# Merge gates of two token blocks computed as ten steps of seven block products between the mLSTM and the merge

## The chip, the cores and the metric

One core of a Trainium2 chip runs the whole kernel. The metric is the time of one execution in microseconds (us); lower is better. A core has five engines: TensorE (PE, matrix products into PSUM), VectorE (DVE), ScalarE (ACT), GpSimd (POOL) and SyncE (SP), which here issues every DMA of the kernel from one queue, in program order.

## The reference, cut to what matters

One layer over 2048 tokens of width 1024. Three mixers (a bidirectional mLSTM, a 2-D neighbourhood attention, a cross-attention into 256 memory tokens) work on one normalised input `h`; sigmoid gates computed from the same `h` merge them; an MLP follows.

```
h = rmsnorm(x, g_mix)
z = h @ w_in                                   # w_in: 1024 x 5648
qk_m, v_m, o_m, i_pre, f_pre, qkv_na, q_mem, gate_pre = split(z)
h_m, h_na, h_mem = mlstm(...), neighbourhood_attention(...), memory_cross_attention(...)
gates = sigmoid(gate_pre).reshape(bsz, s, 3, 1024)   # gate_pre: 3072 of the 5648 columns
y = (gates[:, :, 0] * (h_m @ w_proj_mlstm) + gates[:, :, 1] * (h_na @ w_proj_na)
     + gates[:, :, 2] * (h_mem @ w_proj_mem))
x = x + y @ w_out
return x + square(relu(rmsnorm(x, g_ffn) @ w_up)) @ w_down
```

## The kernel before, in words

Everything is float32. A product is made of three matmuls (`mm3`, L235 to L237): each operand is split into a rounded high part and a low remainder, and high x high, high x low and low x high are added in PSUM. The splits of the weights are an ACT copy and a DVE subtraction (L179/L180 in `fetch`, L205/L206 in `fetch_sums`). Raw weights arrive in tiles `wr`, their split parts are `ws`.

The tokens are four blocks of 512 (b = 0 to 3). `hT` holds one block's normalised input, transposed and split. The PE's order is the program's order; DVE, ACT, POOL and SP are ordered by a scheduler when the program is built, and each then runs in that order. A "tick" is a call between two groups of six matmuls; at each tick, generators ("streams") put in a piece of side work.

Stage one (`phase_1`, `block_a` once for each block) makes the projections of `h`, and its side streams do the attention (`na_stream`) and the memory branch. One attention head of a tile of 128 queries is a score matmul (L1086), a DVE operation that adds the bias and takes the maximum (L1089), an ACT exponential (L1091), a DVE reciprocal and scaling (L1093, L1094), transposes on PE (L1105) and their copy (L1110 on DVE or L1108 on ACT); there are 128 of these. `NA_RATE` says at how many of four ticks a head is put in: one in blocks 0 to 2, two in block 3. The attention's keys, queries, values and biases are loaded from DRAM as `nak`, `naq`, `nav`, `nab`.

A gate unit j (of 24) is 128 columns of the gate weights against one block: 24 matmuls of 128x512, a tanh on ACT (L608) and a store to `s_g`. Blocks 2 and 3 make all their 48 units in stage one (`GATES_1`); blocks 1 and 0 make theirs in stage two, as the filling between the pieces of the mLSTM (`phase_2`, `ml_stream`); what is left of them when the mLSTM is done follows at once (`late_gates`). `sums_down` prepares combinations of the down weights (16 calls, in stage one; loads `xt`, four DVE subtractions L588, stores `s_t`).

Stage three (`phase_3`): for two pairs of blocks, (3, 2) and (1, 0), the merge, the output projection, and the MLP in products of a 2x2 block scheme with seven products instead of eight (`mlp_up`, `mlp_down`). `load_mix` loads a block's three branch outputs (8 DMAs of 512 KB). `X` and `B` hold the operands of the seven products.

The mLSTM runs over 32 chunks (16 in each direction), one in a slot of four ticks, after a start of `START_2` = 20 ticks in which the gates' log-sigmoids (`ml_logsig`) and the first rows of running sums and maxima (`ml_rows`: loads `r_f` and `r_i`, scans L757 and L763, subtractions L766 and L767, PE transposes L784) are made. The seven products of one step stand in `mlp_up` like this (eight would be 96 matmuls, seven are 84):

```
product(c11, "a11", "b11", True)
product(p6, "s2", "t2", True)
product(c12, "s1", "t1", True)
product(c21, "s3", "t3", True)
product(c12, "s4", "b22", False)
product(c11, "a12", "b21", False)
product(c21, "a22", "t4", False)
```

Of the kernel before, what the change touches and what calls it, by code (L numbers as in the profile page):

```python
# [24 lines left out]
TB = 512  # L25
LOW, LATER, LATER_A, SOON = 100, 60, 60, 40
START_2, ROWS_2 = 20, 8
ALONE = 6
CUT = 384
# [3 lines left out]
PREP_V = 2  # L33
MEM_T, MEM_R = 6, 3
NA_LATER, NA_VALUES = 5, 3
# [11 lines left out]
GATES_1, GATES_2 = [2, 3], [1, 0]  # L47
SPILL = [0, 1]
NA_RATE = {0: 1, 1: 1, 2: 1, 3: 2}
# [34 lines left out]
class Body:  # L84
    def __init__(self, tc, a):
# [4 lines left out]
        self.na_ready, self.na_end, self.na_rate, self.tk = [], False, 1, 0  # L90
# [53 lines left out]
    def plan(self):  # L144

        u = unit_index()
        self.down = u["down"]
        out = list(u["w_mem_kv"])
        for b in range(NB):
            for n in ("naqk", "qk", "navm", "v"):  # L150
                out += u[n]
            if b in GATES_1:
                out += u["gate"]
            out += u["o"]
        out += u["gate"] + u["gate"][:ALONE]
        up = [(u["up"][j][0], u["up"][j + 1][0], "sums") for j in range(0, FF // 128, 2)]
        return out + (u["proj"] + u["w_out"] + up) * (NB // 2)

# [132 lines left out]
    def scratch(self):  # L291
# [19 lines left out]
            hT={b: d(f"s_hT{b}", [128, 2, 8, TB]) for b in SPILL},  # L311
            x2=[d(f"s_x2{b}", [TB, D]) for b in range(NB)],
# [62 lines left out]
    def phase_1(self):  # L375
# [7 lines left out]
        self.streams = [self.unit_stream(self.qkq, [(1, 3)]), self.unit_stream(self.memq, [(0,), (2,)]), self.na_stream()]  # L383
# [24 lines left out]
    def prep_x(self, gsrc=None, xt=None):  # L408

        if self.xorder:  # L410
# [81 lines left out]
    def block_a(self, b):  # L492
# [20 lines left out]
        for c in range(4):  # L513
            self.conv(b, c, self.ch_group(self.take(1)[0], hT))
        w = self.take(4)
        zif = self.t("zif", [128, 4, 16], 1)
        for t in range(4):
# [4 lines left out]
            for half in range(2):  # L522
                for r in range(2):
                    p0 = r * 64 + half * 24
                    self.store(self.scr["vna"][half, 8 * b + 2 * t + r], s[p0:p0 + 40])
            p = self.tok_group(hT, w, t, slice(256, 528), 4)
# [4 lines left out]
        for g in {0: [0], 1: [1, 2], 2: [3, 4], 3: [5, 6, 7]}[b]:  # L531
            self.na_ready.append(g)
        self.jobs += [None, None, lambda: self.if_rows(b, zif)]
        w, sums = self.take(4), None
        for t in range(4):
            if t == PREP_V and b + 1 < NB and b not in GATES_1:
# [5 lines left out]
            if b == NB - 1 and t % 2 == 0:  # L542
                sums = sums or self.sums_down(15)
                sums = next(sums, None) and sums
        if b in GATES_1:
            sums, qs = None, list(range(7)) if b + 1 < NB else list(range(7, 15))
            for j in range(24):
                if j == 22 and b + 1 < NB:
                    self.prep_x()
                self.gate(b, j)  # L550
                if j < 21 or b + 1 == NB:
                    if j % 3 != 2:
                        sums = sums or self.sums_down(qs.pop(0))
                        sums = next(sums, None) and sums
        gml = self.gbc[:, b % 2 * TB:(b % 2 + 1) * TB]
        nc.sync.dma_start(gml, a["g_mlstm"])
        w = self.take(4)
        for t in range(4):
# [9 lines left out]
            if b == NB - 1:  # L568
                ts = slice(t * 128, (t + 1) * 128)
                src = self.scr["hT"][GATES_2[0]]  # L570
                if t < 3:
                    nc.sync.dma_start(hT[:, :, :, ts].bitcast(F32), src[:, :, :, ts])
                else:
                    for k in range(0, 8, 2):
                        for l in range(2):
                            nc.sync.dma_start(hT[:, l, k:k + 2, ts].bitcast(F32), src[:, l, k:k + 2, ts])

    def sums_down(self, q):
# [3 lines left out]
        r = [self.x_tile(self.a["w_units"][self.down[half * FF // 256 + q][0]]) for half in range(2)]  # L582
# [1040 lines left out]
```

## Time and profile before

| | |
|---|---|
| time, median of 3 runs | 2893.73 us (2888.53 to 2898.1) |
| profiled execution: time, span | 2894.83 us, 2893.1 us |
| PE busy, weight loads busy | 2861.0 us, 2364.8 us |
| DVE, ACT, POOL busy | 2004.3, 1187.3, 216.4 us |
| DMA | 632.79 MB, mean 219 GB/s |
| stage one, first block of gates in stage two, stage three | from 0, from 938, from 1302 us |

Busy time of PE counts a matmul from its start to a modelled end, and matmuls overlap, so 99% busy does not say that there is nothing to save. What a matmul costs is read from the distance of starts: the profile's rows with `x1` give the start in the first column and the duration in the second.

### The profile page before, as it was taken

How to read it: one execution, taken by the hardware profiler on the slowest of the kernel's cores; microseconds unless marked ns; L12 is line 12 of the kernel's file. 1: busy time of each engine (PE TensorE's matmuls, PEld its weight loads, DVE VectorE, ACT ScalarE, POOL GpSimd, SP SyncE). 2: the span in 40 equal slices, each digit the busy share in tenths (PEclk: the TensorE clock that was granted, in tenths of full speed). 3: DMA queues.
4: the chain of work that ended last, by engine and by line, in shares of the span. 5: the costliest groups of instructions: out<-in, count | busy, mean ns of one | idle time of the engine just before them, and what ended most of it. 6: DMA issues, size and time to landing. Idle time of an engine off the chain costs nothing.

```text
span 2893.1 us, 41875 instructions
## 1 busy us (share of the span) xinstructions
PE 2861.0 (99%) x15052; PEld 2364.8 (82%) x15052; DVE 2004.3 (69%) x3438; ACT 1187.3 (41%) x2256; POOL 216.4 (7%) x382
## 2 busy tenths in 40 slices
PE   8999999999999999999999999999999999999999
PEld 6878788878877888888888888888888888888887
DVE  6676765567765555647598888666785988885666
ACT  7465654344543443532243334443322433344331
POOL 4121310011000122310000000000000000000000
PEclk9999999999999999999999999999999999999999
DMA  8786778877899888978344446656863444476654
GB/s 281 227 270 203 226 231 259 259 222 231 270 306 299 269 258 283 308 261 272 117 137 158 160 146 238 224 189 228 301 205 113 144 148 160 151 249 202 196 188 160
DMA packets 345153, 632.79 MB, mean 219 GB/s; under 512 B 29456, under 2 KB 151248, under 8 KB 344944
## 3 DMA queue, kind: packets, MB, share of 16 engines
q1 hardware_dynamic: 344944, 630.10, 67.5%
q8 instruction: 119, 1.95, 0.3%
q14 instruction: 90, 0.74, 0.1%
HBM read 453.37 MB, written 176.62 MB: 218 GB/s over the span
## 4 chain that ended last, share of the span: by engine, by line
PE 89%; DVE 3%; issue 3%; DMA 3%; ACT 1%; POOL 0%; SPq 0%; DVEq 0%; POOLq 0%; ACTq 0%
PE mm L235 27%; PE mm L237 27%; PE mm L236 27%; PE tr L1105 1%; PE pn L882 1%; PE mx L1086 1%; PE mx L1119 1%; PE pn L885 1%; PE mx L891 1%; DVE ws L180 1%; DMA nav<-s_vna 1%; PE mx L1258 1%; PE tr L1248 1%; DMA xt<-in_xT_dram 0%; DMA wr<-in_w_units_dram 0%
## 5 line engine op out<-in xcount | busy, mean ns | idle before, releaser
L235 PE MATMUL mm<-X,ws 128*128 128x512 f32 x896 | 349.0, 389 | 0.0
L237 PE MATMUL mm<-X,ws 128*128 128x512 f32 x896 | 348.6, 389 | 0.0
L236 PE MATMUL mm<-X,ws 128*128 128x512 f32 x896 | 348.6, 389 | 0.0
L180 DVE TENSOR_TENSOR ws<-wr,ws 128x1024 fp32r<-128x1024 f32 (+1 forms) x194 | 240.0, 1244 | 127.4 <-ACT ws L179 126.2
L235 PE MATMUL mm<-hT,ws 128*128 128x512 f32 (+1 forms) x712 | 283.0, 397 | 0.7 <-ACT ev L565 0.7
L237 PE MATMUL mm<-hT,ws 128*128 128x512 f32 (+1 forms) x712 | 277.0, 389 | 0.0
L236 PE MATMUL mm<-hT,ws 128*128 128x512 f32 (+1 forms) x712 | 276.7, 389 | 0.0
L235 PE MATMUL mm<-ws,hT 128*128 128x512 f32 (+2 forms) x704 | 258.3, 367 | 3.5 <-ACT zif L529 2.7
L237 PE MATMUL mm<-ws,hT 128*128 128x512 f32 (+2 forms) x704 | 249.6, 355 | 2.2 <-DVE hT L438 2.2
L179 ACT ACTIVATE ws<-wr 128x1024 fp32r<-128x1024 f32 (+1 forms) x194 | 204.1, 1058 | 111.1 <-PE mm L237 76.0
L236 PE MATMUL mm<-ws,hT 128*128 128x512 f32 (+2 forms) x704 | 248.7, 353 | 0.0
L237 PE MATMUL mm<-X 128*128 128x512 f32 x616 | 239.7, 389 | 0.2 <-DVE X L1509 0.2
L236 PE MATMUL mm<-X 128*128 128x512 f32 x616 | 239.6, 389 | 0.0
L235 PE MATMUL mm<-X 128*128 128x512 f32 x616 | 239.6, 389 | 0.0
L205 ACT ACTIVATE ws<-wr 128x512 fp32r<-128x512 f32 x224 | 135.0, 628 | 220.1 <-PE mm L237 139.5
L1508 ACT ACTIVATE X<-X 128x1024 fp32r<-128x1024 f32 x109 | 115.6, 1062 | 202.6 <-DMA X<-s_a 67.2
L237 PEld LDWEIGHTS mm<-X,ws 128*128 128x128 f32 x896 | 168.2, 188 | 35.0
L235 PEld LDWEIGHTS mm<-X,ws 128*128 128x128 f32 x896 | 168.2, 188 | 34.9
L236 PEld LDWEIGHTS mm<-X,ws 128*128 128x128 f32 x896 | 168.2, 188 | 34.8
L1509 DVE TENSOR_TENSOR X<-X 128x1024 fp32r<-128x1024 f32 x109 | 132.6, 1223 | 79.0 <-ACT X L1508 78.5
L1535 DVE TENSOR_TENSOR acc<-acc,mm 128x512 f32<-128x512 f32 x192 | 126.5, 683 | 64.8 <-PE mm L237 64.8
L235 PEld LDWEIGHTS mm<-hT,ws 128*128 128x128 f32 x712 | 134.0, 188 | 28.9 <-issue 4.3
(286 smaller groups left out, 5985.6 us busy)
## 6 DMA issues: line engine op xcount, KB each, us to landing
wr<-in_w_units_dram SPq DMA_DIRECT2D x290, 512.0 KB
s_s<-u SPq DMA_DIRECT2D x32, 1024.0 KB
s_g<-ev SPq DMA_DIRECT2D x96, 256.0 KB
ev<-s_g SPq DMA_DIRECT2D x96, 256.0 KB
s_a<-u SPq DMA_DIRECT2D x96, 256.0 KB
X<-s_s SPq DMA_DIRECT2D x45, 512.0 KB
nab<-in_rpb_dram SPq DMA_DIRECT2D x96, 220.0 KB
xt<-in_w_units_dram SPq DMA_DIRECT2D x32, 512.0 KB
```

The source lines that it names most:

```text
L179: nc.scalar.activation(w[:, 0], raw, AF.Copy)
L180: nc.vector.tensor_tensor(w[:, 1], raw, w[:, 0].bitcast(F32), ALU.subtract)
L205: nc.scalar.activation(hi, src, AF.Copy)
L235: mm(out, lhs[0], rhs[0], start=first, stop=False)
L236: mm(out, lhs[0], rhs[1], start=False, stop=False)
L237: mm(out, lhs[1], rhs[0], start=False, stop=last)
L882: mm(pn[h % 2][:, h // 2], pt[:, h], v1[:, h], start=h < 2, stop=first)
L885: mm(pn[h % 2][:, h // 2], qw[hp, h // 2], C[hp, h // 2], start=False, stop=True)
L891: nc.tensor.matmul(pu[hp, h // 2], kw[:, h], v1[:, h], start=True, stop=True)
L1508: nc.scalar.activation(hi, src, AF.Copy)
L1509: nc.vector.tensor_tensor(lo, src, hi.bitcast(F32), ALU.subtract)
L1535: nc.vector.tensor_tensor(c, c, p, ALU.add)
```

## The change

The gate units are placed anew: block 0 keeps its place in stage two, block 3 is made at the end of stage one and in stage two, and most of blocks 1 and 2 is made late, as a pair:

- Stage one makes 4 units (`EARLY`) of blocks 1 and 2 and, at its end, 8 units (`FIRST_3`) of block 3: 16 units instead of 48. Stage two makes 16 units of block 3 and 24 of block 0: 40 instead of 48.
- The other 20 units of blocks 2 and 1 are made after the mLSTM and before the merge, in `pair_gates`: ten steps, each two units against two blocks in seven products of 12 matmuls. Its weights are prepared by `fetch_sums`, as in `mlp_up`; its right-hand operands are made from the normalised input of blocks 1 and 2, which stage one now stores (`s_raw`, 8 DMAs of 512 KB) and which is loaded again in stage two (`load_raw`, 4 DMAs of 1 MB) and combined and split (`gate_operands`: 22 DVE and 14 ACT operations of 128x1024).
- Block 1's spilled `hT` (4 MB out, 4 MB in) is gone; block 0's stays.
- The attention is put in at two of four ticks in blocks 1 to 3, and at three of four in block 3 after its value projection; the order of the projections changes (`navm` ahead of `qk`).
- Of the 16 `sums_down`, 11 stay in stage one (six of them in block 3), five move into `pair_gates`.
- The mLSTM's slots have three ticks, except slots 20 to 31; it starts after 11 ticks, since `ml_logsig` moves to the end of stage one.
- `load_mix` for the first pair moves from the start of stage three into the last steps of `pair_gates`.

In all there are 24 x 40 + 24 x 16 + 10 x 84 = 2184 gate matmuls instead of 2304.

The diff, cut to its core:

```diff
-START_2, ROWS_2 = 20, 8
-ALONE = 6
-CUT = 384
+START_2, ROWS_2 = 11, 0
+FIRST_3, EARLY, ALONE = 8, 4, 4
-NA_LATER, NA_VALUES = 5, 3
+NA_LATER, NA_VALUES, NA_HOLD = {1: 5, 2: 5, 3: 4}, {1: 3, 2: 3, 3: 2}, 3
-GATES_1, GATES_2 = [2, 3], [1, 0]
-SPILL = [0, 1]
-NA_RATE = {0: 1, 1: 1, 2: 1, 3: 2}
+GATES_2, GATES_3 = [3, 0], [2, 1]
+SPILL = [0]
+NA_AT = {1: (3,), 2: (1, 3), 3: (1, 2, 3)}
+NA_RATE = {0: 1, 1: 2, 2: 2, 3: 2}
+SUMS_1 = {0: 1, 1: 2, 2: 2, 3: 6}
...
     def block_a(self, b):
...
+        if b == NB - 1:
+            self.na_rate = 3
...
+        if b == NB - 1:
+            for j in range(FIRST_3):
+                if j == 2:
+                    self.ml_logsig()
+                self.gate(b, j)
+                sum_step()
...
     def late_gates(self, more):
...
+            if i == 1 and new and self.raw is None:
+                self.load_raw()
...
     def ml_stream(self):
...
+            ticks = 3 if slot < 20 or slot >= 32 else 4
...
     def phase_3(self):
...
-        for j in range(2):
-            self.load_mix(order[j], mix[j])
         nc.sync.dma_start(self.gbc, a["g_ffn"])
+        self.jobs += self.gate_operands()
         self.late_gates(lambda: True)
+        while self.jobs:
+            self.tick()
...
+        first[0] = self.pair_gates(order[0], order[1], first[1])
...
+    def load_raw(self):
+        raw = self.p_h.tile([128, 2, 8, TB], F32, name="raw", tag="hT", bufs=1)
+        for h in range(2):
+            for j, b in enumerate(GATES_3):
+                x = raw[:, j, 4 * h:4 * h + 4]
+                self.raw[f"b{h + 1}{2 - j}"] = x
+                self.nc.sync.dma_start(x, self.scr["raw"][b][:, 4 * h:4 * h + 4])
...
+    def gate_operands(self, late=False):
...
+        split("b11", b11)
+        split("b22", b22)
+        op(b12, b22, b12, ALU.subtract)
+        op(b11, b12, b11, ALU.add)
+        split("t2", b11)
+        split("t3", b12)
+        op(b22, b22, b11, ALU.subtract)
+        split("t1", b22)
...
+    def pair_gates(self, b0, b1, mix1):
...
+        for n, j in enumerate(pairs):
+            w, = self.take(1)
+            c11, p6, c12, c21 = (self.ps("mm") for _ in range(4))
+            u2, u3, p5, o11 = (self.ev() for _ in range(4))
+            product(w, c11, "a11", "b11", True)
+            nc.scalar.activation(u2, c11, AF.Copy)
+            if n == len(pairs) - 1:
+                self.load_mix(b1, mix1, (1,))
+            product(w, p6, "s2", "t2", True)
+            add(u2, u2, p6)
+            product(w, c12, "s1", "t1", True)
+            nc.scalar.activation(p5, c12, AF.Copy)
+            if n == len(pairs) - 1:
+                self.load_mix(b1, mix1, (0,))
+            product(w, c21, "s3", "t3", True)
+            add(u3, u2, c21)
+            add(p5, u3, p5)
+            out(p5, c2, j + 1)
+            if sums:
+                next(sums.pop(0), None)
+            product(w, c12, "s4", "b22", False)
...
```

Three places in the built order. The first is SP's queue at the border of stages one and two. Before, the rows' loads `r_f` stand behind the store of the log-sigmoids `s_lf` and three loads of block 0's operand `hB`:

```order
786 L623 DMA hB<-s_hT_156 128x2x512 [waits DMAHW3_49]
787 L623 DMA hB<-s_hT_156 128x2x512 [waits DMAHW4_49]
788 L105 DMA s_lf<-ev_10795 128x128 [waits DMAHW5_49,DVE_49]
789 L105 DMA s_g_93<-ev_10861 128x512 [waits DMAHW6_49,Activation_49]
790 L175 DMA wr_10899<-in_w_units_dram 128x1024 [waits DMAHW7_49]
791 L623 DMA hB<-s_hT_156 128x2x512 [waits DMAHW0_49]
792 L753 DMA r_f<-s_lf 4x512 [waits DMAHW5_49,DMAHW1_49,Pool_49]
```

After, in the same queue:

```order
690 L107 DMA s_t_200<-xt_9503 128x2x512 [waits DMAHW2_49,DMAHW1_49,DVE_49]
691 L107 DMA s_t_200<-xt_9505 128x2x512 [waits DMAHW3_49]
692 L107 DMA s_g_95<-ev_9658 128x512 [waits Activation_49]
693 L181 DMA wr_9728<-in_w_units_dram 128x1024 [waits DMAHW4_49,DVE_49]
694 L181 DMA wr_9771<-in_w_units_dram 128x1024 [waits DMAHW6_49,DMAHW5_49,DVE_49]
695 L774 DMA r_f<-s_lf 4x512 [waits DMAHW3_49,DMAHW7_49,PE_49,Pool_49]
```

The rows' loads now stand right behind the last stores of stage one: a down-weight combination (`s_t`) and the last gate of stage one (`s_g`).

The second is DVE in block 3, where the attention is densest. `nsb` is a head's scores, `npt` its transposed weights, `ws` a weight split, `nho` an output. Before:

```order
1159 L1093 RECIPROCAL sm_9974<-sm_9972 128x1
1160 L1094 TENSOR_SCALAR nsb_9969<-nsb_9969,sm_9974 128x320
1161 L180 TENSOR_TENSOR ws_9912<-wr_9911,ws_9912 128x8x128
1162 L1126 TENSOR_TENSOR nho_9347<-mx_10005,nho_9347 128x4x32
1163 L1110 COPY npt_10032<-tr_10028 120x384
1164 L1089 ISA nsb_10036,sm_10037<-mx_10034,nab_0_1_0_9906 128x320
```

After:

```order
1041 L1122 RECIPROCAL sm_8499<-sm_8497 128x1
1042 L1118 ISA nsb_8518,sm_8519<-mx_8516,nab_0_1_2_8348 128x440
1043 L1118 ISA sm_8519 128x1
1044 L1123 TENSOR_SCALAR nsb_8494<-nsb_8494,sm_8499 128x440
1045 L606 TENSOR_TENSOR xt_8249<-xt_8249,xt_8251 128x512
1046 L1122 RECIPROCAL sm_8523<-sm_8521 128x1
1047 L1118 ISA nsb_8544,sm_8545<-mx_8542,nab_0_1_3_8397 128x440
```

Two heads are now open at a time on DVE, and a subtraction of the down weights (`xt`), which needs a load, stands between them.

The third is DVE late in the mLSTM, where `pt` and `kw` are a chunk's score weights, `og` and `h` the chunk three slots older, `C` the state. Before:

```order
1641 L863 TENSOR_TENSOR kw_2566_13919<-sk_2518_13711,de_2551_13851 128x256 [waits DMAHW0_49,Pool_49]
1642 L866 TENSOR_TENSOR pt_2556_13886<-sk_2518_13711,de_2551_13851 128x512
1643 L926 TENSOR_TENSOR h_2536_13793<-og_13805,rs_13802 128x512 [waits Pool_49]
1644 L924 TENSOR_TENSOR og_13913<-og_13913,h_2561_13901 128x512 [waits DMAHW2_49,DVE_49]
1645 L180 TENSOR_TENSOR ws_13830<-wr_13829,ws_13830 128x8x128 [waits DMAHW3_49,Activation_49]
```

After:

```order
1610 L884 TENSOR_TENSOR kw_2491_12773<-sk_2442_12555,de_2476_12705 128x256 [waits Pool_49]
1611 L887 TENSOR_TENSOR pt_2481_12740<-sk_2442_12555,de_2476_12705 128x512
1612 L1371 TENSOR_TENSOR raw<-raw 128x1024 [waits DMAHW5_49,DMAHW3_49]
1613 L1371 TENSOR_TENSOR raw<-raw 128x1024
1614 L945 TENSOR_TENSOR og_12659<-og_12659,h_2461_12647 128x512 [waits DMAHW7_49]
```

The first operation on the reloaded input (`raw`) stands among the chunk's own operations, and waits for its loads, four of 1 MB each, which stand in a row in SP's queue.

More of the change, by code (lines that the diff above doesn't have):

```diff
@@ L89, in __init__ @@
         self.streams, self.qkq, self.memq, self.aux_end = [], [], [], False
-        self.na_ready, self.na_end, self.na_rate, self.tk = [], False, 1, 0
+        self.na_wait, self.done, self.na_end, self.na_rate, self.tk = list(range(8)), set(), False, 1, 0
+        self.down_q = list(range(16))
         self.na_v, self.na_vfree = [], 2
@@ L311, in scratch @@
             hT={b: d(f"s_hT{b}", [128, 2, 8, TB]) for b in SPILL},
+            raw={b: d(f"s_raw{b}", [128, 8, TB]) for b in GATES_3},
             x2=[d(f"s_x2{b}", [TB, D]) for b in range(NB)],
@@ L541, in block_a @@
             self.store(self.scr["v"][b][t * 128:(t + 1) * 128], s)
[L542 to L548, printed above, removed]
+            if b == NB - 1:
+                sum_step()
+        if b in GATES_3:
+            for j in range(EARLY):
+                if j == EARLY - 2:
                     self.prep_x()
                 self.gate(b, j)
[L551 to L555, printed above, removed]
+                if j < 2:
+                    sum_step()
         nc.sync.dma_start(gml, a["g_mlstm"])
@@ L660, in ml_stream @@
             live[d] = [None if c is None else self.ml_chunk(d, c)] + live[d][:3]
-            for tick in range(4):
-                for age in when[tick]:
+            for tick in range(ticks):
+                for age in when[3 if tick == ticks - 1 else tick]:
                     if age < len(live[d]) and live[d][age]:
                         next(live[d][age], None)
-                if tick < 3:
+                if tick < ticks - 1:
                     next(rows, None)
@@ L1292, in phase_3 @@
                 self.hT = self.p_h.tile([128, 2, 8, TB], F32R, name="yT", tag="hT", bufs=1)
-            yT = [[self.hT[:, l] for l in range(2)], [planes("b21"), planes("t4")]]
+                yT0 = [self.hT[:, l] for l in range(2)]
+            else:
+                yT0 = [planes("t3"), planes("b22")]
+            yT = [yT0, [planes("b21"), planes("t4")]]
             self.ahead = 4
-            self.merge(pair, mix, yT)
+            self.merge(pair, mix if i else first, yT)
             self.out_proj(pair, yT)
```

196 lines of the change are left out of this document (137 added, 59 removed).

## The prediction

> **What bounds the kernel now.** I read the page's busy table first, then the stretches of the stages, then what PE waited for, then the starts of matmuls.
>
> ```profile
> span 2893.1 us, 41875 instructions
> PE 2861.0 (99%) x15052; PEld 2364.8 (82%) x15052; DVE 2004.3 (69%) x3438; ACT 1187.3 (41%) x2256; POOL 216.4 (7%) x382
> ```
>
> A matmul's busy time is modelled and overlaps its neighbours', so 99% says only that PE hardly ever stands still. How little it waits is in the view of waits, for PE alone (total us, times, longest):
>
> ```profile
> PE mx L235 <- ACT ws L179: 7.4, 1, 7.4
> PE mx L1086 <- ACT me L1236: 3.6, 2, 1.8
> PE mx L1086 <- DMA nak<-s_ks: 3.4, 2, 2.2
> PE mm L235 <- ACT zif L529: 2.7, 3, 1.3
> ```
>
> The largest is the start of the program, and all that follow are a few microseconds. The price of a matmul comes from stretches (us, busy us and count of PE, PEld, DVE, ACT, POOL; clock; DMA share; GB/s): stage one, stage two, stage three, then a piece of the MLP with nothing but products, and the busiest 100 us of block 3.
>
> ```profile
> 0.00:937.00 937.00, 914.01 (x5801) 756.47 (x5802) 619.16 (x1370) 484.64 (x1014) 139.63 (x251) 1.00 0.81 252
> 937.00:1302.00 365.00, 363.58 (x2215) 299.31 (x2214) 201.76 (x429) 152.30 (x479) 76.78 (x131) 1.00 0.86 276
> 1302.00:2893.00 1591.00, 1583.37 (x7040) 1309.05 (x7038) 1183.40 (x1640) 550.35 (x765) 0.00 (x0) 1.00 0.56 186
> 1500.00:1800.00 300.00, 300.00 (x1325) 248.43 (x1324) 250.06 (x377) 101.47 (x159) 0.00 (x0) 1.00 0.50 170
> 800.00:900.00 100.00, 96.41 (x634) 78.30 (x635) 65.58 (x159) 46.61 (x99) 3.80 (x27) 1.00 0.98 304
> ```
>
> Products alone: 300 us hold 1325 matmuls that touch the stretch, each 0.39 us long, so the starts are (300 + 0.4) / 1325 = 0.2267 us apart, not 0.389. DVE is 250 of 300 us busy there (83%) with PE never waiting. The granted clock is 1.00 throughout. So PE binds in every stage, and whatever takes matmuls away without a new wait shortens the span at 0.2267 us each.
>
> **The change part by part. Products.** Gate matmuls fall from 2304 to 2184: 120 x 0.2267 = **-27.2 us**. It depends little on where they stand. In stage one a gate with one head in it runs between these two rows (start, duration):
>
> ```profile
> 555.29 0.40 PE L235 MATMUL mm<-hT,ws 128*128 128x512 f32 x1
> 560.80 0.60 PE L1105 MATMUL tr<-ident,nsb 128*120 128x128 f32 x4
> ```
>
> 24 matmuls in 5.51 us, 0.2296 each. Moving 960 of them (40 units) out of stages one and two at 0.2296 and putting 840 back at 0.2267 gives 220.4 - 190.4 = -30.0. The 0.07 us more per gate comes with the head, and the heads stay, so I take -27.2 and keep -30.0 as the far end. The 24 matmuls in two pieces (`CUT`) become whole ones; that is counted. The moved stores, weights and tanhs are as many as before or fewer, except 20 more loads for ten sets of sums against 34 fewer single units; ACT at 41% hides its part.
>
> **Denser attention in block 3.** Stage one loses 32 gates, the cover under which heads run. Per head:
>
> ```profile
> L1091 ACT ACTIVATE nsb<-nsb,sm 128x440 f32<-128x440 f32 (+1 forms) x128 | 81.6, 638 | 94.6 <-DVE sm L1089 92.2 <-DVE halo L684 0.9
> L1089 DVE CUSTOM_DVE_ANT_0 nsb<-mx,nab 128x440 f32<-128x440 f32 (+1 forms) x128 | 73.9, 578 | 58.5 <-PE mx L1086 43.3 <-POOL nsb L1097 8.5 <-DMA nab<-in_rpb_dram 4.3
> L1094 DVE TENSOR_SCALAR nsb<-nsb,sm 128x440 f32<-128x440 f32 (+1 forms) x128 | 55.2, 432 | 3.1
> L1110 DVE COPY npt<-tr 120x512 f32<-120x512 f32 (+1 forms) x64 | 41.7, 652 | 33.0 <-PE tr L1105 32.9
> L1093 DVE RECIPROCAL sm<-sm 128x1 f32<-128x1 f32 x128 | 20.4, 159 | 40.2 <-ACT nsb L1091 39.9
> ```
>
> DVE has 0.578 + 0.432 + 0.159 + 0.652 / 2 = 1.50 us per head. Three heads in four ticks are 24 x 0.2267 = 5.4 us of products and about 2.7 us of the heads' own PE work (0.65 each between the two gates above, from 6.16 us per gate and head, and the values), 8.1 us: one head per 2.7 us, DVE 55% busy with heads. For now, the same stretch 800 to 900 has this many of L1094 (us, DVE busy, count):
>
> ```profile
> 800.00:900.00 100.00, 10.76 (x26) 1.00 0.98 304
> ```
>
> 26 heads, one per 3.85 us, take 39 of DVE's 65.6 us, all else 27. Block 3 lasts from about 600 to 912 us; without 16 of its 24 gates (87 us) and with some heads already done in blocks 1 and 2, I estimate 205 us, so all else would weigh 1.5 times as much, 40%, less 8 weight splits and 3 of 9 sums (8 x 1.24 + 12 x 0.69 = 18 us, 9%): 31%. Together 86%, a little over the 83% under which PE has been seen not to wait. The loads grow as well:
>
> ```profile
> nab<-in_rpb_dram SPq DMA_DIRECT2D x96, 220.0 KB
> nak<-s_ks SPq DMA_DIRECT2D x36, 352.0 KB
> naq<-s_qs SPq DMA_DIRECT2D x48, 128.0 KB
> nav<-s_vna SPq DMA_DIRECT2D x24, 180.0 KB
> ```
>
> A head needs 220 KB of bias, an eighth of 3 x (352 + 128) and a quarter of 180: 445 KB, 0.456 MB: 169 GB/s at 2.7 us against 118 GB/s at 3.85. With the rest as now, 304 GB/s (share 0.98) become some 355. The 48 dense heads last 130 us; 45 GB/s too many are 5.9 MB, 19 us at 304 GB/s. From below it is nothing, as weights are fetched five units ahead and can wait. Between 0 and +19 I take **+5**, nearer the 3.4 us that `nak` costs at 0.98 now.
>
> [...]
>
> **The border of stages one and two.** The rows now start at once instead of 13 us later. Before (start, duration; SP, DVE, PE, POOL):
>
> ```profile
> 951.25 0.35 SPq L753 DMA_DIRECT2D r_f<-s_lf  x1
> 962.15 0.68 DVE L766 TENSOR_TENSOR r_i<-r_i,r_b 36x512 f32<-36x512 f32 x1
> 965.75 0.22 PE L784 MATMUL mx<-ident,r_m 4*128 4x4 f32 x1
> 938.27 0.44 PE L235 MATMUL mm<-hT,ws 128*128 128x384 f32 x1 [0.69 <-ACT ev L565]
> 941.81 0.52 POOL L712 MEMSET r_i<- 36x512 f32 x1 [39.90 <-DMA hT<-s_hT]
> ```
>
> From the issue of `r_f` to the end of L766 it is 11.6 us, then PE may transpose. PE comes to these transposes 11 ticks into the stage, 66 x 0.2267 = 15.0 us. The row tiles are cleared by POOL only when stage one's buffers are free, 3.5 us into the stage before (941.81 - 938.27, waiting for a DMA), and five clearings of 0.5 us follow; `r_f` could be issued about 5 us in and PE served at 16.6: +1.6 us. With the last `s_t` store a few us late it is +6.6; if nothing is late, 0. I take **+3**. PE's own queue stands behind that wait, so the gates wait as well, and `hB`, which now has 8 ticks less to land, profits from it.
>
> **The reloaded input.** DVE's first operation on `raw` stands between two chunks' work and needs 3 of 4 MB that are issued about two slots ahead, when DMA is as full as it gets. 4.2 MB at 304 to 330 GB/s are 13 us, two slots are 13 to 16. Loads of the next chunks queue behind it. Nothing to +6, since a chunk's own loads have a slot of slack; I take **+2**.
>
> **Operands for the first step.** 16 ticks of one DVE operation each, and a first set of sums:
>
> ```profile
> L1509 DVE TENSOR_TENSOR X<-X 128x1024 fp32r<-128x1024 f32 x109 | 132.6, 1223 | 79.0 <-ACT X L1508 78.5
> L206 DVE TENSOR_TENSOR ws<-wr,ws 128x512 fp32r<-128x512 f32 x224 | 151.1, 687 | 1.0
> ```
>
> 16 x 1.22 + 12 x 0.69 = 27.8 us of DVE in the last five gates, 20 ticks or 27.2 us, less what the mLSTM's end still holds; t1 is needed only two products later (5.4 us). 0 to +4, taken as **+1.5**. In the later steps DVE has 12 x 0.69 for sums, five additions and four subtractions, 14.5 of 19.0 us, less than in `mlp_up`: nothing.
>
> **The merge's operands.** Block 2's 4.2 MB are now loaded 11 to 16 us before the steps end, and first used three units (16 us) later. They were loaded early before, in a stretch like this one:
>
> ```profile
> 1300.00:1325.00 25.00, 25.00 (x112) 20.71 (x111) 11.32 (x18) 3.98 (x5) 0.00 (x0) 1.00 0.98 363
> ```
>
> At 363 GB/s they take 12 us, so 27 are enough unless gates and weights crowd them out: 0 to +4, taken as **0**. The mLSTM with slots of three ticks loses an empty tick of four, and a sixth more traffic per time at a share of 0.86: taken as 0, inside the bounds of the reload.
>
> **Sum:** -27.2 + 5 + 3 + 2 + 1.5 = -15.7 against the profiled 2894.8 (span 2893.1), 2879.1. That execution is 1.1 us over the median of 2893.7, so **2878**. All low ends: -30.0, 2864. All high ends: -27.2 + 19 + 6.6 + 6 + 4 + 4 = +12.4, 2906.
>
> **The rivals.** The shift costs next to nothing: the waits come to 3 us or less, as PE's list of today suggests, where even block 3 at 0.98 cost 3.4. Then -24 to -30: about 2867.
>
> Block 3 is bound by transfers: the surplus is not deferred, since SP issues in order and loads of biases stand behind sums' stores. The 19 us come in full: -27.2 + 19 + 3 + 2 + 1.5 = -1.7, 2892. For it: share 0.98 at 304 GB/s; against it: only two waits on `nak`.
>
> Slower: the softmax chain falls behind on DVE. From this row
>
> ```profile
> DVE xt L588 <- DMA xt<-in_w_units_dram: 14.7, 6, 4.6
> ```
>
> DVE already stands up to 4.6 us at a subtraction of the down weights whose load is late, and whatever follows stands with it. Before, 8 ticks lay between a head's scores and its transposes in blocks 0 to 2; now 4 to 6, in which another head opens. If each of the 48 dense heads comes 1 us late, PE waits 48 us and the kernel ends at 2894 - 27 + 48 = 2915. It decides from 0.75 us per head (36 us). Against it: such waits on `xt` have left no mark in PE's list. [...]
>
> That the change does not do what it says can be left out: the built program has 120 full products fewer.
>
> **How the numbers follow.** 0.3% is 8.7 us, about what a measurement of this kernel tells from no change: faster ends at 2885.0, slower begins at 2902.4. The sum's case holds 0.55 (its own range 2869 to 2885), the cheap shift 0.15 (2862 to 2869), the transfers 0.20 (2885 to 2902), the late softmax 0.10 (from 2902). Faster 0.70, same 0.20, slower 0.10. The range 2862 to 2899 leaves out the late softmax (0.10), the last of the transfers' case and a little below.
>
> **What would show it.** Stage one should be 32 x 24 x 0.2267 = 174 us shorter plus block 3's waits; the ten steps 840 x 0.2267 = 190 us. PE's list should name `nak`, `nab` or L1094's successor in block 3, `r_i` at the border, and little within the steps. I am wrong if the steps wait for their sums or operands each time, or if the mLSTM at three ticks makes PE wait in every slot.

## The result, and the profile after

The changed kernel takes 2928.52 us (median of 4 runs, 2925.4 to 2934.63) against 2891.17 for the kernel before on the same chip: ratio 1.0128, 95% interval 1.0102 to 1.0154. It is slower by 37 us, where 2878 us and a gain were forecast. The profiled execution has a span of 2923.7 us, 31 more than before's; it lies 3 us under the median of its kernel, and before's lay 4 us over its own. From its page:

```profile
span 2923.7 us, 41742 instructions
PE 2850.3 (97%) x14908; PEld 2348.0 (80%) x14908; DVE 2086.1 (71%) x3586; ACT 1219.6 (42%) x2326; POOL 216.8 (7%) x382
```

PE has 11 us less busy time in a longer span. The stages, as in the prediction (us, busy us and count of PE, PEld, DVE, ACT, POOL; clock; DMA share; GB/s), and the ten steps last:

```profile
0.00:785.00 785.00, 747.89 (x5033) 615.11 (x5034) 562.96 (x1325) 437.10 (x956) 139.34 (x251) 0.99 0.81 252
785.00:1142.00 357.00, 328.19 (x1995) 265.13 (x1994) 217.28 (x443) 149.74 (x474) 77.46 (x131) 0.98 0.82 265
1142.00:2923.00 1781.00, 1774.21 (x7884) 1467.74 (x7882) 1305.87 (x1819) 632.73 (x896) 0.00 (x0) 1.00 0.55 187
1142.00:1333.00 191.00, 191.00 (x845) 158.19 (x844) 118.76 (x177) 80.61 (x130) 0.00 (x0) 1.00 0.60 208
```

Counted at 0.2267 us a matmul, stage one should end at 938 - 174 = 764 us; it ends at 785, 21 late. Stage two loses eight gates: 363 - 43.5 = 320 us expected, 357 measured, 37 too many. Stage three is where it was forecast, and the ten steps run without a wait. What PE waited for (total us, times, longest):

```profile
PE tr L951 <- DVE h L947: 16.5, 8, 7.3
PE mx L241 <- ACT ws L185: 6.7, 1, 6.7
PE mx L1115 <- DMA nak<-s_ks: 6.3, 3, 4.4
PE tr L1134 <- DVE nsb L1123: 6.2, 3, 2.2
PE mx L865 <- issue: 3.4, 2, 1.9
```

The first row is new, and it is the mLSTM's: L947 makes the normalised `h` of a chunk, L951 transposes it. The third and fourth are attention in stage one (keys not there; a softmax not done, in blocks 1 and 2). Of before's list, the start of the program (second row) and `nak` (3.4 us then) are still there.

### The profile page after: what moved, and what is told of

The parts are those of the page before. It is cut to its first block, busy times and chain, and to the rows that moved or that the text cites. A ratio compares the mean times of both kernels' runs of the same rounds, so it can differ in the third digit from the quotient of the medians.

```text
span 2923.7 us, 41742 instructions
## 1 busy us (share of the span) xinstructions
PE 2850.3 (97%) x14908; PEld 2348.0 (80%) x14908; DVE 2086.1 (71%) x3586; ACT 1219.6 (42%) x2326; POOL 216.8 (7%) x382
## 4 chain that ended last, share of the span: by engine, by line
PE 83%; DVE 6%; DMA 6%; issue 2%; ACT 2%; SPq 1%; POOL 1%; DVEq 0%; ACTq 0%; POOLq 0%
PE mm L241 26%; PE mm L243 25%; PE mm L242 25%; DVE ws L186 1%; PE tr L1134 1%; DMA nak<-s_ks 1%; ACT ws L185 1%; PE pn L903 1%; PE mx L1148 1%; PE mx L1115 1%; DVE cy L711 1%; DMA wr<-in_w_units_dram 1%; DMA wb<-s_w 0%; PE mm L1536 0%; PE pn L906 0%
## 5 line engine op out<-in xcount | busy, mean ns | idle before, releaser
L241 PE MATMUL mm<-X,ws 128*128 128x512 f32 x1032 | 401.8, 389 | 0.0
L243 PE MATMUL mm<-X,ws 128*128 128x512 f32 x1032 | 401.5, 389 | 0.0
L242 PE MATMUL mm<-X,ws 128*128 128x512 f32 x1032 | 401.5, 389 | 0.0
L211 ACT ACTIVATE ws<-wr 128x512 fp32r<-128x512 f32 x294 | 176.8, 628 | 280.6 <-PE mm L243 181.7
L186 DVE TENSOR_TENSOR ws<-wr,ws 128x1024 fp32r<-128x1024 f32 (+1 forms) x160 | 196.7, 1236 | 84.5 <-ACT ws L185 79.1
L241 PE MATMUL mm<-ws,hT 128*128 128x512 f32 (+2 forms) x640 | 233.6, 365 | 5.3 <-ACT zif L538 2.9
L243 PE MATMUL mm<-ws,hT 128*128 128x512 f32 (+2 forms) x640 | 226.8, 354 | 1.9 <-DVE hT L448 1.9
L242 PE MATMUL mm<-ws,hT 128*128 128x512 f32 (+2 forms) x640 | 226.1, 353 | 0.2 <-DVE ws L186 0.2
L243 PEld LDWEIGHTS mm<-X,ws 128*128 128x128 f32 x1032 | 193.7, 188 | 40.2
L242 PEld LDWEIGHTS mm<-X,ws 128*128 128x128 f32 x1032 | 193.7, 188 | 40.2
L241 PEld LDWEIGHTS mm<-X,ws 128*128 128x128 f32 x1032 | 193.8, 188 | 40.0
L185 ACT ACTIVATE ws<-wr 128x1024 fp32r<-128x1024 f32 (+1 forms) x160 | 168.3, 1058 | 103.3 <-PE mm L243 88.6
L212 DVE TENSOR_TENSOR ws<-wr,ws 128x512 fp32r<-128x512 f32 x294 | 198.2, 688 | 1.4
L241 PE MATMUL mm<-hT,ws 128*128 128x512 f32 x384 | 157.2, 409 | 0.7 <-ACT ev L626 0.7
L243 PE MATMUL mm<-hT,ws 128*128 128x512 f32 x384 | 150.6, 392 | 0.0
L242 PE MATMUL mm<-hT,ws 128*128 128x512 f32 x384 | 150.4, 392 | 0.0
```

The source lines that it names most:

```text
L185: nc.scalar.activation(w[:, 0], raw, AF.Copy)
L186: nc.vector.tensor_tensor(w[:, 1], raw, w[:, 0].bitcast(F32), ALU.subtract)
L211: nc.scalar.activation(hi, src, AF.Copy)
L212: nc.vector.tensor_tensor(lo, src, hi.bitcast(F32), ALU.subtract)
L241: mm(out, lhs[0], rhs[0], start=first, stop=False)
L242: mm(out, lhs[0], rhs[1], start=False, stop=False)
```

## The experiments

Ratios are against the kernel before, run on the same chip in the same series. Two marks are read from PE's timeline in each kernel: the last group of value matmuls of the attention (it starts 9 us ahead of the border of the stages in after) and the first product of stage three. Between them lies stage two, 366 us in after, though 371, 371 and 373 in three kernels below that change nothing there (early8, early16, sums_late), and 370 and 374 in two that change only the number of some buffers (sk3, hf3). Block 3 alone varies by 6 us in the same way. One profile thus tells a difference of about 5 us in a stage, not a smaller one.

| kernel | ratio, 95% interval | attention ends | stage three begins | between |
|---|---|---|---|---|
| before | 1 | 917.4 | 1301.7 | 384.3 |
| before_t3 | 1.0079, 1.0062 to 1.0096 | 916.1 | 1324.5 | 408.5 |
| before_steady | 1.0016, 1.0004 to 1.0028 | 916.4 | 1303.9 | 387.5 |
| before_t3_hm | 1.0057, 1.0040 to 1.0074 | 911.7 | 1312.9 | 401.2 |
| after | 1.0128, 1.0102 to 1.0154 | 776.2 | 1142.5 | 366.3 |
| raw_none | 1.0112, 1.0097 to 1.0127 | 774.4 | 1141.9 | 367.5 |
| raw_none2 | 1.0103, 1.0087 to 1.0119 | 781.8 | 1142.7 | 360.9 |
| raw_spread | 1.0110, 1.0088 to 1.0131 | 772.7 | 1136.3 | 363.5 |
| w_half | 1.0110, 1.0095 to 1.0125 | 777.6 | 1143.9 | 366.3 |
| ticks4 | 1.0095, 1.0076 to 1.0114 | 775.7 | 1123.8 | 348.1 |
| early8 | 1.0102, 1.0087 to 1.0117 | 806.3 | 1177.4 | 371.1 |
| early16 | 1.0128, 1.0111 to 1.0145 | 894.9 | 1266.2 | 371.3 |
| sums_late | 1.0112, 1.0095 to 1.0129 | 772.4 | 1145.0 | 372.6 |
| mix | 1.0085, 1.0070 to 1.0100 | 772.0 | 1127.9 | 355.9 |
| mix8 | 1.0077, 1.0062 to 1.0093 | 810.9 | 1166.5 | 355.6 |
| mix_less | 1.0067, 1.0052 to 1.0083 | 777.4 | 1129.4 | 352.0 |

**First theory: the reload of `raw`.** In after PE's longest wait in stage two, 7.3 us from 1061.5 on, comes just behind the four 1 MB loads (issued from 1049.8 to 1053.5), and the chain of work that ended last runs there through `og`, which is queued behind them (start, us). Rival: the mLSTM's slots of three ticks.

```profile
1054.38 12.73 DMA og<-s_o
```

raw_none:

```diff
-                self.nc.sync.dma_start(x, self.scr["raw"][b][:, 4 * h:4 * h + 4])
+                self.jobs += [lambda x=x: self.nc.gpsimd.memset(x, 0.0), None, None, None]
```

> The 4 MB reload of raw is left out: GpSimd fills raw with zeros instead, so the gates of blocks 2 and 1 are wrong; every PE instruction stays. Theory A (the burst): raw's four 1 MB loads stand ahead of the mLSTM's small loads on SP's queue, PE waits 7.4 + 3.7 + 1.9 us for h between 1061 and 1092 and then runs at a granted clock of 0.88 for 60 us (another 7 us); without the load stage two falls from 357 to about 337 us and the kernel by about 20 us, to 2908. Theory B (the slots of three ticks): the shorter slots cost what is lost whatever is loaded; stage two stays above 350 us and the kernel gains 0 to 5 us.

raw_spread (16 pieces through `self.jobs`, `b21` last):

```diff
-                self.nc.sync.dma_start(x, self.scr["raw"][b][:, 4 * h:4 * h + 4])
+                for k in range(4):
+                    loads.append(... x[:, k:k + 1] <- scr["raw"][b][:, 4 * h + k:4 * h + k + 1] ...)
+        for l in loads:
+            self.jobs += [l, None]
```

> The same 4 MB in 16 pieces of 256 KB, one every second tick, between the mLSTM's loads; b21, which is used last, comes last. Theory A in its form of order (the burst delays the small loads behind it): the waits of 7.4 and 3.7 us and the low clock go, the kernel gains 12 to 18 us. Theory A in its form of volume (the queues move about 310 GB/s at a DMA share of 1.0 there, and 4 MB are 13 us more of it wherever they stand): the gain is 0 to 5 us, with the same sum of waits spread over more slots. Theory B: 0 to 3 us.

Both gained next to nothing, inside the intervals. But raw_none had put another wait in the load's place (start, duration, engine):

```profile
1035.84 5.31 POOL L1353 MEMSET raw<- 128x2048 f32 x3
1041.19 1.64 DVE L1371 TENSOR_TENSOR raw<-raw 128x1024 f32<-128x1024 f32 x1 [2.50 <-POOL raw L1353]
```

VectorE stands at L1371 for GpSimd, and the next chunk's `h` behind it. So the load was left out once more with nothing instead; raw_none2 takes the operands from `hB`:

```diff
-        split("b11", b11)
-        split("b22", b22)
-        op(b12, b22, b12, ALU.subtract)
-        op(b11, b12, b11, ALU.add)
+        split("b11", s11)                      # s11, s12, s22: views of hB
+        split("b22", s22)
+        op(b12, s22, s12, ALU.subtract)
+        op(b11, b12, s11, ALU.add)
...
```

> The 4 MB reload is left out and nothing put in its place: the operands of the pair steps are worked out from block 0's h, which is on the chip, with the same instructions on every engine but SP (the gates of blocks 2 and 1 come out wrong). In raw_none GpSimd's memsets (5.3 us for three) stood ahead of rs, for which VectorE and PE wait, so that run didn't price the reload. Theory A (the reload, by order or by volume): the waits of 7.4, 3.7 and 1.9 us between 1061 and 1092 and the clock of 0.88 there go, stage two is 15 to 20 us shorter, near 340. Theory B (slots too short for the chain behind h, whatever is loaded): stage two stays above 350.

w_half (block 0's last twelve gates use each weight unit twice):

```diff
-        self.gq += [(1, j, True, whole) for j in range(both)]
+        self.gq += [(1, j, j % 2 == 0, whole) for j in range(both)]
...
```

> The last 12 late gates, block 0's alone, load every second weight unit and use it twice: 6 units of 512 KB less (3 MB) in the last 65 to 95 us of stage two, with 6 splits on ScalarE and VectorE less (half of block 0's gates 0 to 11 come out wrong). Volume theory (the queues are full there: share 1.0 at 311 to 351 GB/s from 980 to 1080): 3 MB at 0.31 MB per us are 10 us, and the kernel gains 6 to 10. Theory A by order alone: 0 to 3, since the 4 MB of raw still stand ahead of the mLSTM's loads. Theory B: 0 to 2.

Without the reload stage two is 5 us shorter than after's, 10 to 12 shorter than in the three kernels that change nothing there, and the ratio falls by 0.0025 (7 us, but the intervals overlap, so that the price isn't settled). The 7.3 us wait is gone, as PE's row for stage two shows, yet stage two stays at 361: the theory's 15 to 20 us are not there.

```profile
PE tr L951 <- DVE h L947: 9.7, 7, 2.2
```

w_half tells nothing apart: its ratio is lower by 0.0018, inside the intervals, and stage two is as long as after's.

**Second theory: slots of three ticks.** ticks4 gives every slot four again; before_t3 gives the kernel before nothing but the short slots.

```diff
-            ticks = 3 if slot < 20 or slot >= 32 else 4
-            if slot % 8 == 2 and slot < 24:
+            ticks = 4
+            if slot % 8 == 3 and slot < 24:
```

> Every slot of the mLSTM has four ticks again; 163 ticks then stand against 160 of the gates, so that three ticks and the 16 jobs that make the operands have no gates beside them (some 20 us of VectorE work, with PE idle). Theory B (three ticks are too short): the waits within the slots fall from 40 to 10 us or less, and the kernel stays where it is, within 10 us of 2928, since about as much is given back at the end. Theories A and volume: the waits within the slots stay at 25 us or more, and the kernel loses 15 to 25 us.

before_t3, an edit of the kernel before:

```diff
+            ticks = 3 if slot < 20 or slot >= 32 else 4
-            if slot % 8 == 3 and slot < 24:
+            if slot % 8 == 2 and slot < 24:
-            for tick in range(4):
-                for age in when[tick]:
+            for tick in range(ticks):
+                for age in when[3 if tick == ticks - 1 else tick]:
...
```

> The kernel before, with nothing of the change but the mLSTM's slots: three ticks in slots 0 to 19 and from 32 on. Every instruction of PE is the same; only how many gates' products stand between the steps of the mLSTM is less, and the 26 ticks that are saved stand behind it, all gates. Theory B (the chain behind h doesn't come faster than slots of four ticks; what the short slots save, PE waits): PE's waits in stage two rise from 6 us to 25 to 40, and this kernel is 15 to 30 us slower than before. Theories of the reload or of the late weights: neither is changed here, so it stays within 5 us of before.

before_t3 is 23 us slower than before, with the same instructions on PE. First and last of the mLSTM's products in before and in before_t3:

```profile
L882 PE MATMUL pn<-v,pt x256: 272/275/277, 998.3 to 1260.6; 128*128 128x129 f32 x128
```

```profile
L883 PE MATMUL pn<-v,pt x256: 272/275/422, 990.4 to 1250.8; 128*128 128x129 f32 x128
```

262.3 and 260.4 us. Between the two ends stand 744 gate matmuls in before and 630 in before_t3: 19 of the 26 ticks, 25.8 us of products at 6 x 0.2267 a tick, and without them it is 2 us shorter. (Five more ticks are missing ahead of it, and it starts 8 us sooner.) These 24 ticks stand behind it as bare gates: from the last `pn` to stage three it is 41.1 us in before and 73.7 in before_t3. 32.6 - 1.9 - 7.9 = 22.8, the whole loss. In after the same rows give 827.3 to 1100.1, 272.8 us, and in ticks4 832.1 to 1108.0, 275.9: here too the short slots bought 3 us. In ticks4 all gates of stage two are done at 1116, 26 us before after's, and the kernel comes out within 10 us of after, as theory B said, since the end gives most of it back. PE's waits in ticks4 from 785 on, and its stretch 1116 to 1150:

```profile
PE mm L241 <- ACT X L1365: 10.7, 3, 6.9
PE tr L951 <- DVE h L947: 6.6, 5, 4.6
PE mm L242 <- DVE X L1366: 4.2, 3, 2.7
```

```profile
1116.00:1150.00 34.00, 19.15 (x55) 13.58 (x55) 28.29 (x30) 18.05 (x22) 0.00 (x0) 0.70 0.16 47
```

The waits for `h` fall from 16.5 to 6.6 us, and the operands `X`, which now have no gates beside them, take what was won. So what the short slots brought was five gates kept for the operands, and PE paid for them earlier by waiting.

before_steady takes a tick only from eight slots in which no rows are made:

```diff
+            ticks = 3 if 5 <= slot <= 8 or 13 <= slot <= 16 else 4
...
```

> The kernel before with three ticks in the eight slots 5 to 8 and 13 to 16 alone (no rows are made there, and in before_t3 and after these slots ran at 7.1 us without a wait). If short slots cost only where the rows are made and in the second half, the eight ticks are free: the kernel stays within 4 us of before. If the mLSTM as a whole takes some 275 us whatever stands between its steps, the eight ticks are waited out later: 8 to 11 us slower.

4.4 us slower by medians (2898.07 to 2893.7; 1 to 8 by the interval): just past the first case, well under the second. These short slots are nearly free: from the first `pn` to the last it is 253.8 us, 8.5 less than in before for 10.9 us of products less, and those follow as bare gates (52.9 us to stage three against 41.1). So by this profile the chain can go faster in these eight slots, and most of what before_t3 lost it lost in the others; whether by the rows that are made there or by the second half was not tested. Nothing is gained either, since PE never waited there.

**Third question: why the steps can't come faster.** From 1130 to 1275 us ScalarE, GpSimd and VectorE wait in before for (the row with the largest sum of each):

```profile
ACT hf L918 <- DVE h L915: 39.5, 14, 5.4
...
POOL rs L328 <- ACT hf L918: 69.9, 15, 6.8
...
DVE sm L904 <- ACT sm L903: 28.3, 9, 4.5
```

and in before_t3 for (each down to its largest row on a load):

```profile
ACT de L833 <- DMA rb<-s_r: 33.3, 12, 3.9
...
POOL rs L328 <- ACT hf L919: 27.4, 6, 6.2
POOL qw L848 <- DMA wb<-s_w: 26.2, 11, 3.6
...
DVE C L898 <- PE mx L892: 19.3, 8, 4.4
DVE h L916 <- DMA hf<-s_hf: 15.6, 8, 4.5
```

In before the three wait almost only for other engines; all their rows on loads come to 7 us. In before_t3 these come to 85 us: loads are first for ScalarE, and second, close behind another engine, for GpSimd and VectorE. The loads come later than their users want them; it seems that they have lost a lead that they had in before, which the traces don't prove. From 1140 to 1220 the DMA share was at 0.98 in before already (1.00 in before_t3), and PE never stood; before first, then before_t3:

```profile
1140.00:1220.00 80.00, 80.00 (x508) 65.78 (x506) 53.88 (x118) 40.78 (x163) 30.19 (x48) 1.00 0.98 310
```

```profile
1140.00:1220.00 80.00, 76.08 (x475) 61.78 (x473) 51.55 (x114) 38.47 (x149) 26.58 (x45) 1.00 1.00 315
```

Is it buffers, or full queues (a DMA share of 1.00 from 980 to 1080 us in after)? From 970 to 1110 SP stands 18.6 us in after in 8 waits for `pt`, which frees the only buffer that `sk` has in each direction:

```profile
SPq L835 <- DVE pt L887: 18.6, 8, 6.0
```

sk3:

```diff
-        sk = self.t(f"sk{d}", [128, 6, 128], 1) if given or gives else None
+        sk = self.t("sk", [128, 6, 128], 3) if given or gives else None
...
-        og = self.t("og", [128, 512], 3)
+        og = self.t("og", [128, 512], 2)
```

> After, with three shared buffers for the mLSTM's sk (one for each direction in after) and two of three for og, so that it fits; PE's order is the same. Loop theory: SP's queue stands 18.6 us in 8 waits for pt, which frees sk's only buffer (3.0 us in ticks4, 7.2 in before), and the loads behind it (wb, rb, hf, og) come late to the next h; with a buffer free SP's waits for pt fall below 5 us, PE's waits for h from 16.5 to 8 or less, and the kernel gains 8 to 18 us. Transfer theory (the queues are full from 980 to 1080 in any case): the waits only change their names, and the kernel gains 0 to 3 us.

hf3:

```diff
-            hf = self.t(f"hf{d}", [128, 4, 128], 1)
+            hf = self.t("hf", [128, 4, 128], 3)
```

> After, with three shared buffers for hf in place of one for each direction; PE's order is the same. If the load of hf is late because its buffer comes free late, VectorE's waits for hf (1 to 1.7 us in every second slot) go and the kernel gains 3 to 8 us. If it is late because SP issues it late (it stands behind sk, rb and wb) or the queues are full, it gains 0 to 2.

sk3 lies at 1.0128 (1.0109 to 1.0147), hf3 at 1.0130 (1.0108 to 1.0152): nothing gained. In sk3 SP's waits for `pt` from 970 to 1110 are gone, but another row of its list, 16.9 us in after, has grown, and in all SP waits 44.2 us there against 49.8:

```profile
SPq L107 <- DVE hm L956: 22.4, 11, 5.3
```

PE's waits for `h` stay at 15.2 us (16.5 in after). The loop theory falls. Then the volume. before_t3_hm stores half of each chunk's output:

```diff
-        self.store(self.scr["hm"][b][:, :, cs], hm.rearrange("p l h t -> p (l h) t").bitcast(F32))
+        self.store(self.scr["hm"][b][:, 0:4, cs], hm[:, 0].bitcast(F32))
...
```

> before_t3 with half of each chunk's mLSTM output stored (the high halves alone, 256 KB of 512; the merge reads them twice, so its output is off by the low halves): 4 MB of some 25 MB less in the mLSTM's second half, where the DMA share is 1.0 and, unlike in before, ScalarE waits 33 us for rb, GpSimd 26 us for wb and VectorE 16 us for hf. Transfer theory (the loads have lost their lead and the queues are too full to win it back): those waits fall by half or more, and of the 23 us that before_t3 lost 8 to 13 come back. Chain theory (the steps themselves take that long): 0 to 3 us come back.

It is 6 to 8 us faster than before_t3 (by ratios, by medians), from the first `pn` to the last it is 253.1 us in place of 260.4, and PE's waits for `h` fall from 11.2 to 5.2 us (before_t3's row first). But the waits of the other engines for loads, which the transfer theory wanted halved, come to 85 us again (the rows on loads last):

```profile
PE tr L931 <- DVE h L927: 11.2, 6, 5.3
```

```profile
PE tr L931 <- DVE h L927: 5.2, 4, 3.3
```

```profile
ACT de L833 <- DMA rb<-s_r: 26.6, 11, 3.5
...
POOL qw L848 <- DMA wb<-s_w: 23.0, 10, 3.4
...
DVE h L916 <- DMA hf<-s_hf: 20.6, 7, 5.1
```

That lies between the two theories, with intervals that overlap: traffic seems to have a part, some third of the 23 us for 4 MB; it isn't shown to be all. Why the steps can't come faster stays open.

**Attention in stage one.** early8 and early16 put gates of blocks 2 and 1 back (in early16 all 16 sums go to stage one too); sums_late takes four sums out; rate2 thins block 3.

```diff
-FIRST_3, EARLY, ALONE = 8, 4, 4
+FIRST_3, EARLY, ALONE = 8, 8, 4                # early8; 8, 16, 4 in early16
```

> EARLY = 8: four more gates of each of blocks 2 and 1 go back to stage one, and eight pair steps are left of ten (5.4 us of products given back). Theory C (attention is too dense in stage one: 20 us of waits and low clock there): stage one grows by less than the 43.5 us of eight gates, by 32 to 36, and the kernel gains 2 to 6 us. Rival (stage one loses by the new order in block 0 and by what stands at the block ends, whatever the gates beside it): stage one grows by 43 us and the kernel loses 5 us.

> EARLY = 16: twelve more gates of each of blocks 2 and 1 go back to stage one, four pair steps are left of ten (16.3 us of products given back), and all 16 sums are made in stage one. In early8 eight gates more lengthened stage one by 30.1 us up to the end of attention, where they are 43.5 us of PE's time: 13 us of waits were covered. Theory C (only density costs): 24 gates (130.6 us) lengthen it by 110 to 114, all 20 us come back, and the kernel lies at 2921 to 2927. Rival (the first eight gates took what could be had): it lengthens by 117 or more, and the kernel lies at 2930 to 2936.

Eight gates (43.5 us) move the end of attention by 30.1 us, so that 13 us of PE's losses were covered: its waits in stage one fall by 7 us and its time at half clock by 14, which is 7 us of work (128x512 matmuls start 0.43 us apart at half clock and 0.23 at full, as the last section shows). The mean of the three kernels with these eight gates (mix8 and mix8sk below) and of the ten with after's stage one moves by 33.0, so some 10 us are the safer figure. The kernel is 7 us faster by ratio, with intervals that overlap, though it gives back 5.4 us of products. By the first 128x272 matmul of each block, block 1 grew by 13.5 us for 21.8 us of gates, block 2 by 19.3; mix8 has nearly the same (208.0 and 209.5 us for the two blocks, 208.2 and 207.2 in early8, 194 to 197 and 186 to 189 in the ten). So what was covered lay in block 1, where a head stands in every second tick, as in block 2. The next 16 gates (87.1 us) move it by 88.6: nothing more is to be had, as early16's rival said.

```diff
-SUMS_1 = {0: 1, 1: 2, 2: 2, 3: 6}
+SUMS_1 = {0: 1, 1: 0, 2: 0, 3: 6}
```

> SUMS_1 of blocks 1 and 2 from 2 each to 0: four sums of the down projection's operands (VectorE work and 1 MB of loads each) go from stage one to the pair steps. Theory D (VectorE is late with the softmax at the block ends, where PE waits for nsb 2 us at a time): stage one is shorter by 4 to 10 us. Rival (the waits come from how close the heads stand, or from transfers): stage one is within 2 us of 785. The pair steps pay 0 to 4 us for the sums, which end later there.

Attention ends 3.8 us sooner than in after, inside the 771.7 to 781.8 us of the ten kernels with after's stage one: not told apart.

```diff
-            self.na_rate = 3
+            self.na_rate = 2                       # and FIRST_3 = 13
```

> Attention in block 3 at two heads of four ticks again (three in after), with FIRST_3 = 13 gates beside it at the end of stage one; stage two then has 35 gates, too few for the mLSTM and the operands, so that only stage one is to be read. By PE's work alone the border of the stages moves 27.2 us (five gates) to 812.5. Theory C for block 3 (density there costs the 8 to 10 us that PE waits in it): the border comes at 802 to 806. Rival (block 3 waits for its transfers at any rate): 811 to 815.

One execution alone: the first matmul on `hB`, which both kernels have five gates into stage two, comes at 839.8 us against 816.1, so the border is 23.7 us later for 27.2 us of gates, at 809. That lies between the two cases, which one profile can't tell apart; density in block 3 isn't shown to cost more than 4 us.

**Put together.** mix has short slots only where they are cheap and one gate more in stage two; mix8 adds EARLY = 8 and a reload in eight pieces; mix8sk adds sk3's buffers; mix_less is mix without the reload and with half the last weights.

```diff
+            ticks = 3 if 5 <= slot <= 8 or 13 <= slot <= 16 or slot >= 32 else 4
...
-FIRST_3, EARLY, ALONE = 8, 4, 4
+FIRST_3, EARLY, ALONE = 7, 4, 4                # mix; 7, 8, 4 in mix8
```

> Three ticks only in slots 5 to 8 and 13 to 16, where the slots of after ran at 7.1 us without a wait, and from 32 on; four elsewhere; FIRST_3 = 7, so that 164 ticks of gates stand against 149 of the mLSTM, and 15 of the 16 operand jobs keep a gate beside them. Theory B: the waits in stage two fall to some 15 us as in ticks4, the operands no longer cost the 24 us that PE waited or ran slow for them there, and the kernel gains 18 to 26 us, to 2902 to 2910. Theory A: the reload's waits stay, the kernel gains 0 to 8 us.

> mix with EARLY = 8 (as early8, 5.4 us of products given back, 13 us of waits covered in stage one) and the reload in 8 pieces, one every second tick. If the causes add: 5 us below mix for early8 and 2 to 5 for the reload, 2892 to 2902: level with before or up to 8 us above it. If the waits of both stages are one limit that moves along (transfers), mix8 equals mix within 3 us.

> mix8 with the buffers of sk3. Loop theory: mix8's waits for h (12.7 us) and the low clock behind them go, and the kernel gains 8 to 15 us on mix8's 2918.6: 2904 to 2911. Transfer theory: within 3 us of mix8.

> mix without the reload (as raw_none2) and with every second weight unit of the last 11 late gates used twice (as w_half): 4 + 2.5 MB less from 1030 us on; the gates concerned come out wrong. Transfer theory: the waits of mix between 1030 and 1085 (13 us, and a clock of 0.89 behind them) go, and the kernel comes to 2900 to 2910. Chain theory: it stays within 4 us of mix, at 2918 to 2925.

mix gains 12 us on after by ratio, clear of the intervals but less than forecast; stage two is 10 us shorter, and between 1020 and 1090 PE still waits:

```profile
PE tr L951 <- DVE h L947: 12.3, 5, 3.9
```

mix8 is level with mix (2918.57 to 2921.63 us), and mix8sk with mix8 (1.0087, 1.0067 to 1.0106), so the gains don't add. mix_less gains 5 us more on mix (the intervals overlap), where transfers alone would have given 12 to 22: at most a part again. No version run here beats the kernel before; the nearest of those that do the whole work of the change is mix8, 0.8% behind.

## Why the prediction was wrong, point by point

- **Products, -27.2: right.** From the first matmul of the ten steps to the first behind them it is 190.4 us, 840 x 0.2267, without a wait.
- **Operands of the first step, +1.5, and the merge's, 0: right.** Stage three is 0.6 us shorter than its matmuls' count gave.
- **The reload, +2 (0 to +6): probably sized too low.** raw_none2 puts it at 7 us by ratio, with intervals that overlap, and at 5 to 12 by its stage.
- **The border, +3:** what can be read there is 1.3 us for `hB` and 3.4 at L865 in all of stage two; about right, not tested alone.
- **The mLSTM at three ticks, "taken as 0, inside the bounds of the reload": the step that failed.** It counted a slot as the PE work in it, so that a tick less is 1.36 us less. The mLSTM took 262.3 us with four ticks and 260.4 with three, for 25.8 us of products less in between; before_t3 shows that this alone costs 23 us. The prediction's last sentence named it as what would make it wrong, yet gave it no term, no price and no rival. The row to see was DMA at 0.86 over stage two: with the prediction's own sixth more traffic per time that is 1.00, and from 1140 to 1220 us it was at 0.98 already. That the loads alone set the length of a slot isn't shown.
- **Denser attention, +5 in block 3: mis-sized and misplaced.** Stage one lost 21 us; 10 to 13 of them came back with eight gates, in block 1. The estimate was made for the three-in-four rate of block 3 and took blocks 1 and 2, which lost their gates too, at nothing.
- **The rivals.** The slower one (2915 us) came nearest in time by another mechanism: PE did wait for the softmax, 6.2 us in all, not 48. Block 3 bound by transfers: 6.3 us of waits for `nak`, not 19.

Where the time went on PE can be added up from the two profiles. The rows of PE's waits come to 66.9 us in after and 26.0 in before, and half the length of its stretches at half clock to 20.7 and 4.4. That is 40.9 and 16.3 more; less 27.2 of products it is 30.0 of the 30.6 us that the span grew (some 2 us at half clock fall into waits and are counted twice). Stage one has 13.9 and 6.8 of it, stage two 27.4 and 8.5, which are the 21 and 37 us lost there. So waits and half clock are the whole loss.

What stays open is what caused a part of these waits. The slots cost 23 us in before_t3 and the reload about 7 in raw_none2; if the two add, some 7 of stage two's 37 us are without a cause that a run shows, and so are 8 to 11 of stage one's 21.

## What to carry to other kernels

Where one engine's work fills the gaps of a chain on others, ask how long the chain takes without the filling before thinning it: filling taken out of a chain that is at its own speed comes back behind it as bare work (41.1 us of it in before, 73.7 in before_t3). A transfer share near 1.0 without waits is no proof of room: here, from 1140 to 1220 us, a share of 0.98 stood beside no wait of PE in before, and one of 1.00 beside PE busy for 76.1 of 80 us once the filling was thinned, with 85 us of waits for loads on three engines from 1130 to 1275. Filling that is moved away from one place is missed there: count the cover of each block, not only of the densest one (eight gates put back won 10 to 13 us, in block 1).

## What the runs showed of the hardware

In after two waits of PE cost more than themselves. The stretch of the 7.3 us wait, then the two stretches at half clock, around the end of this wait (1068.8) and around that of the next one of 3.5 us, which ends at 1081.3 (the third figure from the right is the granted clock):

```profile
1061.00:1068.50 7.50, 0.48 (x3) 0.06 (x1) 4.19 (x5) 0.00 (x0) 0.00 (x0) 0.84 1.04 378
1066.10:1072.90 6.80, 4.13 (x22) 3.71 (x24) 1.72 (x3) 1.17 (x4) 0.51 (x1) 0.50 1.00 305
1079.80:1086.60 6.80, 5.34 (x29) 4.59 (x30) 2.27 (x4) 3.90 (x16) 2.85 (x4) 0.50 1.05 360
```

The clock falls within the wait, 2.7 and 1.5 us ahead of its end, and stays at half behind it for 4.1 and 5.3 us. The eight `pn` matmuls in each stretch take 1.86 us from their first start to the next group's, against 0.99 at 1037.1, where the granted clock is 1.00:

```profile
1037.08 1.06 PE L903 MATMUL pn<-v,pt 128*128 128x129 f32 x8
1038.07 0.71 PE L906 MATMUL pn<-C,qw 64*128 64x129 f32 x8
...
1069.65 1.93 PE L903 MATMUL pn<-v,pt 128*128 128x129 f32 x8
1071.51 1.23 PE L906 MATMUL pn<-C,qw 64*128 64x129 f32 x8
```

In the kernel before a wait of 1.8 us that ended at 312.6 had half clock behind it too, from 314.1 on (128x512 matmuls start 0.43 us apart there and 0.23 from 317.7 on); one of 2.2 us that ended at 878.0 had none:

```profile
309.00:314.00 5.00, 3.17 (x44) 2.45 (x43) 4.50 (x11) 4.01 (x11) 1.73 (x2) 1.00 0.99 297
314.10:317.50 3.40, 3.40 (x12) 2.71 (x11) 1.44 (x5) 2.21 (x9) 2.93 (x3) 0.50 1.01 320
...
876.00:880.00 4.00, 2.04 (x10) 1.76 (x10) 1.17 (x6) 0.73 (x3) 0.00 (x1) 1.00 1.05 390
```

The stretch at half clock is 3.4 us long behind the 1.8 us wait and 6.8 us around the ends of those of 7.3 and 3.5 us. What makes the clock fall, and for how long, these rows don't show. Over the whole span the mean granted clock is 0.998 in before and 0.993 in after: 0.7% of 2923.7 us less 0.2% of 2893.1 is 14.7 us more, part of which falls within the waits themselves; so by this estimate up to half of the 31 us that the span grew is clock that went with the waits.
